# Attention values for two heads at once: 512 columns, one buffer of transposed probabilities

## The chip, the core and the metric

The kernel runs on one core of one Trainium2 chip. The metric is the device time of one execution in microseconds. TensorE (PE) multiplies matrices, VectorE (DVE), ScalarE (ACT) and GpSimd (POOL) compute element by element, SyncE (SP) issues most DMA transfers. PSUM holds the products of TensorE, in eight banks of 128 partitions x 512 fp32; SBUF holds everything else on the chip, DRAM the rest.

## The reference

One layer of an encoder, for two sequences (`s` = 0 and 1) of 1024 positions with 1024 features. The part around the change is latent attention with four heads: scores from a part without position and a rotary part, a softmax over 1024 keys, and the product with the values. Its output and that of a Fourier branch go through one projection, are added to the input, normalised, and feed a feed-forward network.

```python
sc = (jnp.einsum('bqhd,bkhd->bhqk', qn_b, k_nope)
      + jnp.einsum('bqhr,bkr->bhqk', qp_b, k_pe)).astype(jnp.float32) * scale
p = jax.nn.softmax(sc, axis=-1).astype(v.dtype)
return jnp.einsum('bhqk,bkhd->bqhd', p, v)
...
mix = jnp.concatenate([y_mla, y_four], axis=-1) @ w_out
x = x + ga1 * mix
h2 = rmsnorm(x, g_ffn) * (1.0 + sc2) + sh2
ffn = (jax.nn.silu(h2 @ w_gate) * (h2 @ w_up)) @ w_down
```

## The kernel before

A number is split into a high and a low part of type fp32r (`split`, L61: ScalarE casts to the high part at L62, VectorE subtracts it to give the low part at L63), and a product is made of three matmuls: high x high, high x low, low x high (`mm3`, L78, L79, L80). The key and value projections are folded into the queries and into the output weights, so that the values of a head are products with the common latent `ckv` of 128 features.

The stage of the change is the loop over `k` at the end of the attention part. `items` has 64 entries (s, b, h, u): sequence, block of 256 queries (`b`, four in a sequence), head, half of the block (`u`, 128 queries). So eight iterations make one block. An iteration issues:

- `scores(k)`: ten matmuls of 512 columns into two PSUM banks (`ps_s`, two buffers), the maximum on VectorE (L1012), the exponential on ScalarE (L1015), the scaling by the inverse sum (L1017). The result is `p`.
- at fixed places of the eight, the queries of the next block: `rope_q`, `rope_flip` (tile `pqt`), `absorb_q` (tile `qa`), six matmuls of 256 columns each for the first and last;
- `flip_p(k - 1)`: eight transposes of 128 columns (L1033) into two PSUM buffers (`tbank`, tile `ppt`), each split into the transposed probabilities `pt`. `pt` has two parts (high, low) of eight chunks of keys x 256 queries of one head, in two buffers each;
- `values`, in every second iteration, for the head whose halves were flipped: 24 matmuls of 256 columns into `po` (tile `gb`, two buffers of one bank shared with the queries and the output products), split into `o`;
- `out_step`, from k = 11 on, for the block that is finished, by `i` = 0 to 7: loads of two times 128 rows of `fo_d` (the Fourier branch with the input added, `out_load`), four output products of 12 matmuls of 512 columns (`out_proj`, i = 0 to 3), each added by VectorE (L945), the store of the sum and its normalisation (`norm2`, i = 1 and 3), and the transposition of the normalised rows into `h2_d` (`flip_h`, tile `pht`, i = 3 and 5), which takes the same two `tbank` buffers and eight operations on ScalarE (L975);
- the entries of `todo`: the splits of the output weights `wv` (k = 3 to 10 for the first sequence, 39 to 42 for the second), accumulating transfers of the input into `fo_d` on POOL's queue (`add_x`), combinations for the next stage (`comb_h`, k = 49 to 59), loads.

The last two blocks are handled apart: the output products of block (1, 2) are issued in iterations 64 to 67, those of block (1, 3) in the next stage, behind the last values.

The order of each engine's instructions isn't that of the text alone. The program is laid out by a scheduler that plays the engines through with assumed durations: instructions stand in the order in which it finds them ready, with those of earlier iterations first. So transposes whose source isn't ready let later products go ahead. `issue_after` and `first` put single operations behind others.

Of the kernel before, what the change touches and what calls it, by code (L numbers as in the profile page):

```python
# [12 lines left out]
F32 = mybir.dt.float32  # L13
F32R = mybir.dt.float32r
# [7 lines left out]
P = 128  # L22
# [12 lines left out]
NOUT = 6  # L35
# [17 lines left out]
def hybrid_encoder_kernel(ctx: ExitStack, tc: tile.TileContext, a: dict):  # L53
    nc = tc.nc

    here = {}

    def rd(t):
        return t.bitcast(F32)

    def split(hi, lo, src):  # L61
        here["a"] = nc.scalar.copy(hi, src).ins  # L62
        here["v"] = nc.vector.tensor_tensor(out=lo, in0=src, in1=rd(hi), op=ALU.subtract).ins  # L63
# [13 lines left out]
    def mm3(out, lh, ll, rh, rl, first, last, cont=False):  # L77
        nc.tensor.matmul(out, lh, rh, start=first, stop=False, skip_group_check=cont)  # L78
        nc.tensor.matmul(out, lh, rl, start=False, stop=False, skip_group_check=cont)  # L79
        nc.tensor.matmul(out, ll, rh, start=False, stop=last, skip_group_check=cont)  # L80
# [83 lines left out]
    with ExitStack() as st:  # L164
        p1b = st.enter_context(ExitStack())
        w2 = p1b.enter_context(tc.tile_pool(name="p1b", bufs=1, side="right", reuse_waits="tile"))
        w = st.enter_context(tc.tile_pool(name="p1", bufs=1, reuse_waits="tile"))
# [444 lines left out]
    S = {}  # L612
# [65 lines left out]
    def absorb_q(s, b, h, bankf):  # L678
        ql = S["q", s, b]
        pq = bankf()  # L680
        hs = slice(h * P, h * P + P)
        for c in range(2):
            mm3(pq[:, :256], wq_h[:, c, hs], wq_l[:, c, hs], ql[0][:, c, :], ql[1][:, c, :], c == 0, c == 1)
        qa = qa_tiles()
        split(qa[0], qa[1], pq[:, :256])
        S["qa", s, b, h] = qa
# [21 lines left out]
    with ExitStack() as st:  # L708
        early = st.enter_context(ExitStack())
        wa = early.enter_context(tc.tile_pool(name="p2a", bufs=1, reuse_waits="tile"))  # L710
        w = st.enter_context(tc.tile_pool(name="p2", bufs=1, side="right", reuse_waits="tile"))
# [175 lines left out]
        for s in range(2):  # L887
            for n in range(8):
                g, j = n // 4, (1, 2, 3, 0)[n % 4]
# [31 lines left out]
    tail = ExitStack()  # L921
    tl = tail.enter_context(tc.tile_pool(name="p4", bufs=1, side="right", reuse_waits="tile"))
# [6 lines left out]
    def tbank(name, dt=F32):  # L929
        return tl_ps.tile([P, 4, P], dt, tag="t", name=name, bufs=2)  # L930

    def out_load(s, b, u):
        r0 = (2 * b + u) * P
        x2 = tl.tile([P, D], F32, tag="x2", name="x2", bufs=2)
        nc.sync.dma_start(x2, fo_d[s][r0 : r0 + P, :])
        S["x2", s, b, u] = x2

    def out_proj(s, b, u, g):
        o, x2 = S["o", s, b], S["x2", s, b, u]
        us = slice(u * P, u * P + P)  # L940
        gs = slice(512 * g, 512 * g + 512)
        pm = gbank()
        for h in range(HEADS):
            mm3(pm, o[0][:, h, us], o[1][:, h, us], wv[0][:, h, gs], wv[1][:, h, gs], h == 0, h == HEADS - 1)
        here["v"] = nc.vector.tensor_tensor(out=x2[:, gs], in0=x2[:, gs], in1=pm, op=ALU.add).ins  # L945

    def norm2(s, b, u, pool, later=False):
        r0 = (2 * b + u) * P
        x2 = S.pop(("x2", s, b, u))
        (nc.gpsimd if (s, b) == (1, 2) else nc.sync).dma_start(x2_d[s][r0 : r0 + P, :], x2)  # L950
        ms = tiny.tile([P, 2], F32, name="ms2")
        xn = pool.tile([P, D], F32, tag="xn", name="xn", bufs=1)
        sq = nc.scalar.activation(xn, x2, AF.Square, scale=1.0 / 32.0, accum_out=ms[:, 0:1]).ins
        r = rstd(ms[:, 0:1], 1)
        S["xn", s, b, u] = xn

        def scale():
            here["n"] = sq, nc.vector.tensor_scalar(out=xn, in0=x2, scalar1=r[:, 0:1], scalar2=None, op0=ALU.mult).ins

        if later:  # L960
            S["scale"] = scale
        else:
            scale()

    def flip_h(s, b, u):
        r0 = (2 * b + u) * P
        xn = S.pop(("xn", s, b, u))
        for g in range(2):
            ht = tl.tile([P, 4, P], F32, tag="ht", name="ht", bufs=2)
            pt = tbank("pht")  # L970
            for c in range(4):
                nc.tensor.transpose(pt[:, c, :], xn[:, (4 * g + c) * P : (4 * g + c + 1) * P], ident)
            for c in range(4):
                cc = 4 * g + c
                nc.scalar.activation(ht[:, c, :], pt[:, c, :], AF.Identity,  # L975
                                     bias=sh2[s][:, cc : cc + 1], scale=s2[s][:, cc : cc + 1])
            nc.sync.dma_start(h2_d[s][:, 4 * g : 4 * g + 4, r0 : r0 + P], ht)

    def out_step(s, b, i):
        if i == 0:  # L980
            out_load(s, b, 0)
            out_load(s, b, 1)
        if i < 4:
            out_proj(s, b, i // 2, i % 2)
        if i in (1, 3):
            norm2(s, b, i // 2, tl, True)
        if i in (3, 5):
            flip_h(s, b, i // 4)

    with ExitStack() as st:  # L990
        w = st.enter_context(tc.tile_pool(name="p3", bufs=1, side="right", reuse_waits="tile"))
# [28 lines left out]

        def flip_p(s, b, h, u):
            p = S.pop(("p", s, b, h, u))
            if (s, b, h, u) == (0, 0, 0, 0):
                w.tile([P, 8], F32, name="phase_pt")
            if u == 0:
                S["pt", s, b, h] = [w.tile([P, 8, 2, P], F32R, tag=f"pt{k}", name=f"pt{k}", bufs=2) for k in range(2)]
            if (s, b, h, u) == (0, 0, 0, 0):
                w.tile([P, 120], F32, name="phase_l")
            pth, ptl = S["pt", s, b, h]
            for g in range(2):  # L1030
                pt = tbank("ppt")
                for c in range(4):
                    nc.tensor.transpose(pt[:, c, :], p[:, (4 * g + c) * P : (4 * g + c + 1) * P], ident)  # L1033
                split(pth[:, 4 * g : 4 * g + 4, u, :], ptl[:, 4 * g : 4 * g + 4, u, :], pt)

        def values(s, b, h):
            ckv = S[s][1]
            pth, ptl = S.pop(("pt", s, b, h))
            if h == 0:
                S["o", s, b] = [tl.tile([P, HEADS, 256], F32R, tag=f"o{i}", name=f"o{i}b{s}{b}", bufs=3) for i in range(2)]  # L1040
            o = S["o", s, b]
            po = gbank()
            for c in range(8):
                mm3(po[:, :256], ckv[0][:, c, :], ckv[1][:, c, :], pth[:, c], ptl[:, c], c == 0, c == 7)
            split(o[0][:, h, :], o[1][:, h, :], po[:, :256])

        items = [(s, b, h, u) for s in range(2) for b in range(4) for h in range(HEADS) for u in range(2)]
        nit = len(items)
# [48 lines left out]
        for k in range(nit + 4):  # L1097
            if k >= nit:
                i = k - nit
                out_proj(1, 2, i // 2, i % 2)  # L1100
                S["tail", i] = here["v"]
                if i == 1:
                    norm2(1, 2, 0, tl)
                    S["tail", 5], S["tail", 6] = here["n"]
            if k < nit:
                s, b, h, u = items[k]
                scores(s, b, h, u)
                if "scale" in S:
                    with tc.issue_after(here["nb"]):
                        S.pop("scale")()  # L1110
                if k == nit - 1:
                    with tc.issue_after(here["exp"]):
                        nc.scalar.activation(tiny.tile([P, 1], F32, tag="pc", name="warm"), cmask[:, 0:1], AF.Silu)
                nxt = items[k + 8 - k % 8] if k + 8 - k % 8 < nit else None
                i = k % 8
                if nxt is not None:
                    if i == 0:
                        load_q(*nxt[:2])
                    if i == 3 and nxt[1] == 0:
                        load_seq(nxt[0], [w.tile([P, 2, N], F32R, tag=f"lat1{i}", name=f"lat1{i}") for i in range(2)])  # L1120
                    if i in (3, 4):
                        rope_q(*nxt[:2], i - 3, gbank)
                    if i in (5, 6):
                        rope_flip(*nxt[:2], i - 5, tbank("pqt", F32R))
                if u == 1 and k + 1 < nit:
                    absorb_q(*items[k + 1][:3], gbank)
            if 0 <= k - 1 < nit:
                flip_p(*items[k - 1])
                if k == nit:
                    S["tail"] = here["a"], here["v"]  # L1130
            if 0 <= k - 3 < nit and (k - 3) % 2 == 1:
                values(*items[k - 3][:3])
                if k == nit + 2:
                    S["tail", 4], S["tail", 7] = here["v"], here["a"]
            m = k - 11
            if 0 <= m < 8 * NOUT:
                out_step(*divmod(m // 8, 4), m % 8)
            for f in todo.get(k, ()):
                f()

    with ExitStack() as st:
# [171 lines left out]
        for s in range(2):  # L1313
# [241 lines left out]
            m, me = {}, {}  # L1555
# [223 lines left out]
```

## Time and profile before

| | |
|---|---|
| median of 3 runs | 2050.19 us (2047.45 to 2050.26) |
| the profiled execution | 2048.8 us, of which its span 2047.0 |
| granted TensorE clock, mean | 0.993 |
| TensorE busy | 1989.8 us (97%) |
| VectorE, ScalarE, GpSimd busy | 1416.4, 902.3, 835.3 us |
| attention stage, first scores to last values | 313.98 to 743.89 us |

A row of the profile's groups has the line, the engine, the operation, output and inputs by the program's names, shapes and the count; then busy time, the mean of one in ns, and the engine's idle time before them with what ended it. A row in order of time has start, duration, engine, line and what it makes. Busy times by stretch have for each engine the time and in brackets the number of operations, then the granted clock, the share of the DMA engines and what they moved.

### The profile page before, as it was taken

How to read it: one execution, taken by the hardware profiler on the slowest of the kernel's cores; microseconds unless marked ns; L12 is line 12 of the kernel's file. 1: busy time of each engine (PE TensorE's matmuls, PEld its weight loads, DVE VectorE, ACT ScalarE, POOL GpSimd, SP SyncE). 2: the span in 40 equal slices, each digit the busy share in tenths (PEclk: the TensorE clock that was granted, in tenths of full speed). 3: DMA queues.
4: the chain of work that ended last, by engine and by line, in shares of the span. 5: the costliest groups of instructions: out<-in, count | busy, mean ns of one | idle time of the engine just before them, and what ended most of it. 6: DMA issues, size and time to landing. Idle time of an engine off the chain costs nothing.

```text
span 2047.0 us, 28668 instructions
## 1 busy us (share of the span) xinstructions
PE 1989.8 (97%) x9994; PEld 1650.2 (81%) x9994; DVE 1416.4 (69%) x2098; ACT 902.3 (44%) x1761; POOL 835.3 (41%) x1026
## 2 busy tenths in 40 slices
PE   5999999999999999999999999999999999999997
PEld 2788878888888887888888888877788888888876
DVE  2667757666677669878777576677766666667674
ACT  2656635555565555333333365454233333336441
POOL 1455213111313316879779410332654454410142
PEclk7999999999999999999999999999999999999999
DMA  9685694544643465546546587674432222358662
GB/s 368 204 268 188 216 341 138 128 87 104 170 104 121 157 240 200 192 156 219 187 159 210 170 295 258 214 233 148 135 113 103 99 107 103 103 186 276 225 224 88
DMA packets 182509, 370.36 MB, mean 181 GB/s; under 512 B 18972, under 2 KB 58396, under 8 KB 179292
## 3 DMA queue, kind: packets, MB, share of 16 engines
q1 hardware_dynamic: 163228, 308.88, 45.1%
q0 software_dynamic: 19136, 59.65, 9.7%
q8 instruction: 78, 1.28, 0.3%
q14 instruction: 67, 0.55, 0.1%
HBM read 256.46 MB, written 120.39 MB: 184 GB/s over the span
## 4 chain that ended last, share of the span: by engine, by line
PE 53%; DVE 3%; DMA 2%; issue 1%; POOL 1%; ACT 0%; SPq 0%; DVEq 0%; ACTq 0%; POOLq 0%
PE bank L79 18%; PE bank L78 18%; PE bank L80 18%; DVE wl L63 2%; DVE val L138 1%; DMA draw<-t_d 1%; POOL val L138 0%; ACT wh L62 0%; DMA rgu<-in_wgu_dram 0%; DVE val L1578 0%; POOL rs_y L106 0%; DMA draw<-s_d 0%; DVE val L1552 0%; DMA draw<-in_w_down_dram 0%; DMA val<-x_d 0%
## 5 line engine op out<-in xcount | busy, mean ns | idle before, releaser
L78 PE MATMUL bank<-H,wh 128*128 128x512 f32 x1224 | 477.4, 390 | 7.1 <-DVE val L138 6.4
L80 PE MATMUL bank<-H,wl 128*128 128x512 f32 x1224 | 476.4, 389 | 0.2 <-DVE wl L63 0.2
L79 PE MATMUL bank<-H,wh 128*128 128x512 f32 x1224 | 476.2, 389 | 0.0
L138 DVE TENSOR_TENSOR val<-bank,val 128x512 f32<-128x512 f32 x244 | 166.7, 688 | 162.0 <-PE bank L80 157.8
L78 PEld LDWEIGHTS bank<-H,wh 128*128 128x128 f32 x1224 | 229.8, 188 | 58.4 <-DVE val L138 7.3
L80 PEld LDWEIGHTS bank<-H,wl 128*128 128x128 f32 x1224 | 229.8, 188 | 49.1 <-DVE wl L63 1.5
L79 PEld LDWEIGHTS bank<-H,wh 128*128 128x128 f32 x1224 | 229.8, 188 | 47.2
L63 DVE TENSOR_TENSOR wl<-draw,wh 128x512 fp32r<-128x512 f32 x286 | 203.4, 744 | 84.9 <-ACT wh L62 84.6
L62 ACT CAST wh<-draw 128x512 fp32r<-128x512 f32 x286 | 169.4, 621 | 158.6 <-PE bank L79 85.3
L79 PE MATMUL bank<-wl,wh 128*128 128x512 f32 x572 | 223.8, 391 | 2.7 <-DVE wl L63 2.7
L138 POOL TENSOR_TENSOR val<-val 128x512 f32<-128x512 f32 x58 | 83.0, 1440 | 347.6 <-DVE val L1552 191.3
L78 PE MATMUL bank<-wh 128*128 128x512 f32 x572 | 222.7, 389 | 0.1
L80 PE MATMUL bank<-wh,wl 128*128 128x512 f32 x572 | 222.7, 389 | 0.0
L62 ACT CAST wh<-rgu 128x512 fp32r<-128x512 f32 x171 | 106.5, 624 | 249.2 <-PE bank L79 195.1
L63 DVE TENSOR_TENSOR wl<-val,wh 128x512 fp32r<-128x512 f32 x133 | 140.5, 1058 | 71.7 <-ACT wh L62 71.3
L63 DVE TENSOR_TENSOR wl<-rgu,wh 128x512 fp32r<-128x512 f32 x171 | 170.0, 995 | 6.9 <-ACT wh L62 6.9
L62 ACT CAST wh<-val 128x512 fp32r<-128x512 f32 x133 | 82.5, 623 | 181.0 <-PE bank L79 156.4
L135 POOL TENSOR_TENSOR val<-rgu 128x512 f32<-128x512 f32 x80 | 112.7, 1409 | 98.0 <-DMA rgu<-in_wgu_dram 94.3
L79 PEld LDWEIGHTS bank<-wl,wh 128*128 128x128 f32 x572 | 107.4, 188 | 28.6 <-DVE wl L63 6.7
L78 PEld LDWEIGHTS bank<-wh 128*128 128x128 f32 x572 | 107.4, 188 | 23.0 <-ACT wh L62 0.7
L80 PEld LDWEIGHTS bank<-wh,wl 128*128 128x128 f32 x572 | 107.4, 188 | 22.1
L1012 DVE TENSOR_REDUCE mx<-ps_s 128x1 f32<-128x1024 f32 x64 | 78.2, 1222 | 61.3 <-PE ps_s L1007 60.8
(385 smaller groups left out, 4092.2 us busy)
## 6 DMA issues: line engine op xcount, KB each, us to landing
rgu<-in_wgu_dram SPq DMA_DIRECT2D x86, 512.0 KB
draw<-s_d SPq DMA_DIRECT2D x143, 256.0 KB
s_d<-val POOLq DMA_DIRECT2D x88, 256.0 KB, 4.2
draw<-t_d SPq DMA_DIRECT2D x88, 256.0 KB
s_d<-val SPq DMA_DIRECT2D x66, 256.0 KB
draw<-in_w_down_dram SPq DMA_DIRECT2D x55, 256.0 KB
wada<-in_w_ada_dram SPq DMA_DIRECT2D x13, 1024.0 KB
xt<-in_x_dram SPq DMA_DIRECT2D x16, 512.0 KB
```

What stands on the lines that cost most here:

```text
L62: here["a"] = nc.scalar.copy(hi, src).ins
L63: here["v"] = nc.vector.tensor_tensor(out=lo, in0=src, in1=rd(hi), op=ALU.subtract).ins
L78: nc.tensor.matmul(out, lh, rh, start=first, stop=False, skip_group_check=cont)
L79: nc.tensor.matmul(out, lh, rl, start=False, stop=False, skip_group_check=cont)
L80: nc.tensor.matmul(out, ll, rh, start=False, stop=last, skip_group_check=cont)
L135: return eng.tensor_tensor(out=out, in0=x, in1=y, op=ALU.subtract).ins
L138: return eng.tensor_tensor(out=out, in0=x, in1=y, op=ALU.add).ins
L1012: nc.vector.tensor_reduce(out=mx, in_=ps, axis=AX.X, op=ALU.max)
```

## The change

`values` takes two heads (`q` = 0 or 1, heads 2q and 2q + 1) at once. A pair's transposed probabilities have four tiles, high and low for each half `g` of the keys, each of four chunks x 512 columns (two heads x two halves), with one buffer each instead of two: the same memory as before. Its 24 matmuls have 512 columns and fill a whole PSUM bank; there are half as many. They are issued where k mod 4 is 1, ahead of `flip_p`, so that the products of a pair stand before the first flip of the next pair. The output steps of a block, which took eight iterations in a row, are spread over i = 9 to 19, counted from the block's own first iteration: loads at 9 and 11, products at 10, 12, 15 and 16, normalisations at 12 and 16, flips at 14 and 19. None of the products falls on an iteration with values. Two small tiles that only moved addresses go away.

```diff
     def out_step(s, b, i):
-        if i == 0:
-            out_load(s, b, 0)
-            out_load(s, b, 1)
-        if i < 4:
-            out_proj(s, b, i // 2, i % 2)
-        if i in (1, 3):
-            norm2(s, b, i // 2, tl, True)
-        if i in (3, 5):
-            flip_h(s, b, i // 4)
+        if i in (9, 11):
+            out_load(s, b, i // 2 - 4)
+        if i in (10, 12, 15, 16):
+            n = (10, 12, 15, 16).index(i)
+            out_proj(s, b, n // 2, n % 2)
+        if i in (12, 16):
+            norm2(s, b, i // 4 - 3, tl, True)
+        if i in (14, 19):
+            flip_h(s, b, int(i == 19))
...
         def flip_p(s, b, h, u):
             p = S.pop(("p", s, b, h, u))
-            if (s, b, h, u) == (0, 0, 0, 0):
-                w.tile([P, 8], F32, name="phase_pt")
-            if u == 0:
-                S["pt", s, b, h] = [w.tile([P, 8, 2, P], F32R, tag=f"pt{k}", name=f"pt{k}", bufs=2) for k in range(2)]
-            if (s, b, h, u) == (0, 0, 0, 0):
-                w.tile([P, 120], F32, name="phase_l")
-            pth, ptl = S["pt", s, b, h]
+            if h % 2 == 0 and u == 0:
+                S["pt", s, b, h // 2] = [[w.tile([P, 4, 4, P], F32R, tag=f"pt{k}{g}", name=f"pt{k}{g}", bufs=1) for k in range(2)]
+                                         for g in range(2)]
+            i = 2 * (h % 2) + u
             for g in range(2):
+                pth, ptl = S["pt", s, b, h // 2][g]
                 pt = tbank("ppt")
                 for c in range(4):
                     nc.tensor.transpose(pt[:, c, :], p[:, (4 * g + c) * P : (4 * g + c + 1) * P], ident)
-                split(pth[:, 4 * g : 4 * g + 4, u, :], ptl[:, 4 * g : 4 * g + 4, u, :], pt)
-
-        def values(s, b, h):
+                split(pth[:, :, i, :], ptl[:, :, i, :], pt)
+
+        def values(s, b, q):
             ckv = S[s][1]
-            pth, ptl = S.pop(("pt", s, b, h))
-            if h == 0:
+            pts = S.pop(("pt", s, b, q))
+            if q == 0:
                 S["o", s, b] = [tl.tile([P, HEADS, 256], F32R, tag=f"o{i}", name=f"o{i}b{s}{b}", bufs=3) for i in range(2)]
-            o = S["o", s, b]
+            o = [t[:, 2 * q : 2 * q + 2, :].rearrange("p h t -> p (h t)") for t in S["o", s, b]]
             po = gbank()
             for c in range(8):
-                mm3(po[:, :256], ckv[0][:, c, :], ckv[1][:, c, :], pth[:, c], ptl[:, c], c == 0, c == 7)
-            split(o[0][:, h, :], o[1][:, h, :], po[:, :256])
+                pth, ptl = (t[:, c % 4].rearrange("p i t -> p (i t)") for t in pts[c // 4])
+                mm3(po, ckv[0][:, c, :], ckv[1][:, c, :], pth, ptl, c == 0, c == 7)
+            split(o[0], o[1], po)
...
+            if (k % 4 == 1 and 5 <= k < nit) or k == nit + 2:
+                values(*divmod(k // 8 - (k % 8 == 1), 4), k // 4 % 2 ^ 1) if k < nit else values(1, 3, 1)
+                if k == nit + 2:
+                    S["tail", 4], S["tail", 7] = here["v"], here["a"]
             if 0 <= k - 1 < nit:
                 flip_p(*items[k - 1])
                 if k == nit:
                     S["tail"] = here["a"], here["v"]
-            if 0 <= k - 3 < nit and (k - 3) % 2 == 1:
-                values(*items[k - 3][:3])
-                if k == nit + 2:
-                    S["tail", 4], S["tail", 7] = here["v"], here["a"]
-            m = k - 11
-            if 0 <= m < 8 * NOUT:
-                out_step(*divmod(m // 8, 4), m % 8)
+            for n in (k // 8 - 1, k // 8 - 2):
+                if 0 <= n < NOUT:
+                    out_step(*divmod(n, 4), k - 8 * n)
```

How the order of instructions moves is shown at three places. First TensorE, around the values of the third head of the first block (before). `gb` is the product, `pt` the transposed probabilities, `ppt` a transposition, `ps_s` scores:

```order
L1007 MATMUL ps_s<-lat_3363,qp 128x512
L78 MATMUL gb<-pt_3962,ckv_3385 128x256
L79 MATMUL gb<-pt_3963,ckv_3385 128x256
L80 MATMUL gb<-pt_3962,ckv_3386 128x256
L78 MATMUL gb<-pt_3962,ckv_3385 128x256
L1033 MATMUL ppt<-ident,p 128x128 x8
L79 MATMUL gb<-pt_3963,ckv_3385 128x256
L80 MATMUL gb<-pt_3962,ckv_3386 128x256
```

The same engine with the change, at the end of the values of heads 2 and 3 of that block:

```order
L78 MATMUL gb<-pt_3962,ckv_3385 128x512
L79 MATMUL gb<-pt_3963,ckv_3385 128x512
L80 MATMUL gb<-pt_3962,ckv_3386 128x512
L1031 MATMUL ppt<-ident,p 128x128 x8
L1003 MATMUL ps_s<-lat_3362,qa_4147 128x512
L1004 MATMUL ps_s<-lat_3363,qa_4147 128x512
```

Before, the transposes of the next half stood inside the run of value products; now they stand behind it, ahead of scores.

Second ScalarE, near a run of values. Before, late in the stage (`o0b` is the cast of the values, `pt` that of the transposed probabilities, `p` the exponential, `qa` a query):

```order
L1015 ACTIVATE p,sm<-ps_s,nb 128x1024
L62 CAST o0b_8236<-gb 128x256
L62 CAST qa_8295<-gb 128x256
L62 CAST pt_8299<-ppt 128x4x128 x2
L1015 ACTIVATE p,sm<-ps_s,nb 128x1024
L62 CAST pt_8299<-ppt 128x4x128 x2
L1015 ACTIVATE p,sm<-ps_s,nb 128x1024
```

With the change, in the second block:

```order
L1015 ACTIVATE p,sm<-ps_s,nb 128x1024
L62 CAST o0b_4438<-gb 128x512
L62 CAST pt_4736<-ppt 128x4x128
L62 CAST pt_4738<-ppt 128x4x128
L62 CAST pt_4736<-ppt 128x4x128
L62 CAST pt_4738<-ppt 128x4x128
L1015 ACTIVATE p,sm<-ps_s,nb 128x1024
```

Behind the cast of the values there now stand the casts of two flips in a row, of the first two items of the next pair, and then the next exponential.

Third TensorE, around the flip of normalised rows (`pht`). Before (`gb<-wv` are output products):

```order
L79 MATMUL gb<-wv_3638,o0b_3892 128x512
L80 MATMUL gb<-wv_3637,o1b_3893 128x512
L972 MATMUL pht<-ident,xn 128x128 x8
L1003 MATMUL ps_s<-lat_3362,qa_4519 128x512
L1004 MATMUL ps_s<-lat_3363,qa_4519 128x512
L1005 MATMUL ps_s<-lat_3362,qa_4520 128x512
```

With the change (`gb<-wq` are query products):

```order
L972 MATMUL pht<-ident,xn 128x128 x4
L78 MATMUL gb<-wq_h,ql_4630 128x256
L79 MATMUL gb<-wq_l,ql_4630 128x256
L972 MATMUL pht<-ident,xn 128x128 x4
L80 MATMUL gb<-wq_h,ql_4631 128x256
L78 MATMUL gb<-wv_3637,o0b_4438 128x512
L79 MATMUL gb<-wv_3638,o0b_4438 128x512
L80 MATMUL gb<-wv_3637,o1b_4439 128x512
L78 MATMUL gb<-wv_3637,o0b_4438 128x512
L1031 MATMUL ppt<-ident,p 128x128 x4
```

The two halves of this flip stood together, with all scores of an iteration behind them; now query products lie between them, and transposes of probabilities follow after four output products.

## The prediction

> **What bounds the kernel now.** I read the page first, then busy time by stretch, then the TensorE groups and the order of time in the stage that is changed.
>
> ```profile
> span 2047.0 us, 28668 instructions
> PE 1989.8 (97%) x9994; PEld 1650.2 (81%) x9994; DVE 1416.4 (69%) x2098; ACT 902.3 (44%) x1761; POOL 835.3 (41%) x1026
> PEclk7999999999999999999999999999999999999999
> PE 53%; DVE 3%; DMA 2%; issue 1%; POOL 1%; ACT 0%; SPq 0%; DVEq 0%; ACTq 0%; POOLq 0%
> ```
>
> TensorE is busy all the time, at a full granted clock after the first slice, and the chain that ended last is made of TensorE. The change lies in the attention stage, the 64 iterations of the loop over `items`. From its first scores at 313.98 us to the last product of values at 743.89 us it takes 429.9 us. Busy time by stretch (the 11 first iterations; two times 8 of the middle; the 8 where the second sequence sets in; the last):
>
> ```profile
> core 0: us, PE busy (x) PEld busy (x) DVE busy (x) ACT busy (x) POOL busy (x), PEclk, DMA share, GB/s
> 313.98:370.62 56.64, 54.43 (x337) 47.34 (x336) 46.11 (x85) 32.20 (x61) 15.56 (x16) 0.97 0.40 108
> 394.50:449.70 55.20, 54.99 (x349) 48.90 (x348) 36.62 (x71) 30.04 (x64) 8.40 (x20) 1.00 0.43 97
> 449.70:504.90 55.20, 54.99 (x349) 48.90 (x348) 36.63 (x71) 30.04 (x64) 8.46 (x20) 1.00 0.43 97
> 574.69:631.49 56.80, 55.87 (x351) 48.77 (x350) 41.26 (x79) 33.79 (x73) 8.99 (x21) 1.00 0.46 112
> 694.95:743.89 48.94, 48.35 (x311) 43.18 (x310) 34.25 (x59) 26.71 (x51) 8.99 (x12) 1.00 0.63 230
> ```
>
> Eight iterations cost 55.20 us, with VectorE busy for 36.6 of them. A busy TensorE is not yet a TensorE at its pace, since matmuls overlap: one that is listed with 0.39 us is followed by the next after 0.23. So I count by starts (first and last of a run of equal products).
>
> ```profile
> 433.32 0.39 PE L1003 MATMUL ps_s<-lat,qa 128*128 128x512 f32 x1
> ...
> 435.36 0.39 PE L1007 MATMUL ps_s<-lat,qp 128*128 128x512 f32 x1
> ...
> 436.31 1.03 PE L1033 MATMUL ppt<-ident,p 128*128 128x128 f32 x8
> 437.10 0.37 PE L78 MATMUL gb<-pt,ckv 128*128 128x256 f32 x1
> 437.30 0.28 PE L79 MATMUL gb<-pt,ckv 128*128 128x256 f32 x1
> ...
> 439.89 0.28 PE L80 MATMUL gb<-pt,ckv 128*128 128x256 f32 x1
> ```
>
> Nine steps of 512 columns take 2.04 us, 0.227 us each; 22 steps of 256 columns take 2.59 us, 0.1177 each. Eight transposes take 0.79 us to the next product, which then is 0.08 us longer than usual: 0.87 us. For 8 iterations of the middle that is 80 scores (18.1 us), 96 value products (11.3), 48 output products (10.9), 80 transposes (8.7), 36 query products of 256 columns (4.2) and two small flips (0.7): 54.0 us. The other 1.2 us of the 55.20 are waits of TensorE. Where they are, in order of time:
>
> ```profile
> 462.67 0.28 PE L80 MATMUL gb<-ql,wq_l 128*128 128x256 f32 x1
> 462.79 0.60 PE L1033 MATMUL ppt<-ident,p 128*128 128x128 f32 x4
> 463.14 0.36 PE L78 MATMUL gb<-pt,ckv 128*128 128x256 f32 x1
> 463.56 0.66 PE L1033 MATMUL ppt<-ident,p 128*128 128x128 f32 x4
> ```
>
> One value product starts at 463.14, and the four transposes behind it start 0.42 us later instead of 0.12. They had been put into a run of value products, and their source or their PSUM buffer wasn't ready.
>
> **The change part by part.**
>
> *512 columns.* The value products:
>
> ```profile
> L78 PE MATMUL gb<-pt,ckv 128*128 128x256 f32 x256 | 73.4, 287 | 0.0
> L80 PE MATMUL gb<-pt,ckv 128*128 128x256 f32 x256 | 72.6, 283 | 0.0
> L79 PE MATMUL gb<-pt,ckv 128*128 128x256 f32 x256 | 72.4, 283 | 0.0
> ```
>
> 768 of these become 384 with 512 columns. Two small ones step 0.2354 us, a large one 0.227: 0.0084 x 384 = 3.2 us less, all of it on TensorE, which is the path. The Trainium skill (TensorE: Matmul & The Clock Gate, Back-to-back issue gap) gives a warm gap of columns / 2.4 + 2.5 ns; an estimate by it is 2.5 ns saved for each pair, 1.0 us in all, and the sum would be 2.2 us smaller. The measured steps are 8 to 11 ns above that rule, so I keep the rows.
>
> *Waits inside the value products.* In the order, the transposes no longer stand in a run of value products; now a whole run of 24 stands by itself and the transposes behind it. In the middle 1.2 us per 8 iterations are waits, over 6.6 such stretches (11 to 63) 7.9 us. I take half of this, 4.0 us, as gone. Why not all: the flips of the normalised rows (`pht`) share two PSUM buffers (`tbank`) with those of the probabilities, and they move into iterations 3 and 6 of 8, where both kinds follow each other closely. Each of these flips keeps ScalarE for eight operations.
>
> ```profile
> L975 ACT ACTIVATE ht<-pht,sh,s 128x128 f32<-128x128 f32 x16 | 5.9, 469 | 2.9 <-PE pht L972 2.8
> L62 ACT CAST pt<-ppt 128x512 fp32r<-128x512 f32 x16 | 8.9, 596 | 7.9 <-PE ppt L1033 7.8
> L1012 DVE TENSOR_REDUCE mx<-ps_s 128x1 f32<-128x1024 f32 x8 | 9.8, 1223 | 9.9 <-PE ps_s L1007 9.8
> L63 DVE TENSOR_TENSOR pt<-ppt,pt 128x512 fp32r<-128x512 f32 x17 | 11.2, 683 | 0.5 <-ACT pt L62 0.3
> ```
>
> 16 of them busy ScalarE for 5.9 us, 0.37 each. In the order of before, scores and a query product (3.0 us) lie between a flip and the next transposes; now 1.7 to 2.4 us do, and four of these operations alone take 1.5. So I expect about 0.2 us of wait for each of two flips in 8 iterations, 2.6 us of the 7.9 over the stage, and a little beside. Bounds: all 7.9 go, or they double (+7.9).
>
> *One buffer of transposed probabilities.* The first flip of the next pair may be written only after the value products have read the pair before. It stands behind them on TensorE anyway, so its cast is never ready earlier: cost 0. The other side is the products' own wait for the last flip before them: a cast (0.596 us), a subtraction (0.683). Between the two the order puts output products and scores (12 x 0.227 + 10 x 0.227 = 5.0 us); that is the cover. In the first ten iterations only scores and a query product are there, about 2 us, and I expect a few tenths. Without cover each of the 16 pairs would cost up to 1.28 us.
>
> *Output products and their DMAs.* Their number stays. Loads of `fo_d` rows move from i = 0 (k = 8n + 11) to k = 8n + 9 and 8n + 11, the stores of `x2_d` and `h2_d` move back, on SP's queue. The first load needs the second accumulating transfer of POOL's queue:
>
> ```profile
> 361.16 0.89 POOL L622 DMA_DIRECT2D fo_d<-in_x_dram  x1
> 368.40 0.81 SPq L935 DMA_DIRECT2D x<-fo_d  x2
> ```
>
> SP waits there until 368.40, and the first addition on VectorE would now come some 3 us earlier than before. At worst it waits for the load, with a split of `wv` and the next maximum behind it, while TensorE has scores: 0 to 2 us once, I take 0. The second split of `wv` (iterations 39 to 42) now follows the last output products of sequence 0 at once; its casts stand behind those of the flips on ScalarE, so nobody waits. Where it used to meet iterations without any product, 56.80 us stood for 55.20. I don't count that 1.6 us, it is in the range.
>
> *The end.* The last split of values is now twice as large:
>
> ```profile
> 744.09 0.38 ACT L62 CAST o0b<-gb 128x256 fp32r<-128x256 f32 x1 [3.65 <-PE gb L80]
> 744.50 0.42 DVE L63 TENSOR_TENSOR o1b<-gb,o0b 128x256 fp32r<-128x256 f32 x1 [0.34 <-ACT o0b L62]
> 744.84 0.68 DVE L135 TENSOR_TENSOR H<-rgu 128x512 f32<-128x512 f32 x1
> ```
>
> VectorE goes straight on with the sums for the next stage, and TensorE waits for it there later. With 0.596 and 0.683 in place of 0.38 and 0.42 this is 0.5 us more. The 12 output products behind the last value products (2.7 us) still hide it from the projection of the last block.
>
> *Sum:* -3.2 - 4.0 + 0.5 = -6.7 us. The profiled execution took 2048.8 us: 2042.1. The median shown is 1.4 us above that execution, so for a median I say 2043.5.
>
> **The rivals.**
>
> *Only the columns count.* The waits go from value products to flips and stay 7.9 us. For it: they come from VectorE's and ScalarE's chain, which loses little work, and the order is planned with other durations than the chip's. Against it: the runs of 24 give 5.4 us in one piece in which both engines catch up. Time: -3.2 + 0.5 = -2.7, 2047.5.
>
> *The single buffer stops TensorE.* Slower. If a cast of the new pair stands first in ScalarE's queue, waiting for the value products, the exponentials behind it wait too; and if the products wait for the last cast and subtraction, all 16 pairs pay 1.28 us, 20.5 us: -2.7 + 20.5 = +17.8, 2068. It decides as soon as less than 1.28 us of TensorE work lies between the last flip of a pair and the first value product. The Trainium skill (TensorE: Matmul & The Clock Gate, Architectural detail) calls ScalarE's and VectorE's queues strictly first in, first out; this speaks against the change. Against this rival: in the order 5.0 us lie there, and the exponential of the scores ahead of the products stands before the waiting casts, not behind them. A milder form, flips that wait 1.0 us each in place of 0.2, twice in 8 iterations, costs 6.6 x 1.6 = 10.6 us above the forecast: 2054.
>
> *The handover eats it.* The next stage begins with waits on VectorE; if its loads, not the end of attention, set them, some of the 6.7 are lost. They shift with the stage, since their buffers are freed by it. Time: between 2044 and 2050, with the first rival.
>
> That the program doesn't do it is no rival: the order shows the runs of 24 with 512 columns and the output products spread.
>
> **How the numbers follow.** About 0.2% (4.1 us) is what a measurement of this kernel can tell from no change. Forecast (2038 to 2046): 0.60. Only the columns, or the gain lost in the handover (2046 to 2054): 0.27. Slower by either form of the single-buffer or flip waits: 0.13. Lower end: all 7.9 and the 1.6 go: -3.2 - 9.5 + 0.5 = -12.2, 2038; I give 2037. Upper end 2053, where the slower case begins; that leaves about 0.15 above and a little below.
>
> **What would show it.** The value products: x128 for each of L78, L79 and L80, steps of 0.227 us. Scores of the middle, 8 iterations apart: 54.2 us instead of 55.2. No transposes inside a run of value products; ScalarE's and VectorE's waits for TensorE at flips about the same. Wrong would be: 8 iterations still at 54.8 or more (the first rival), or value products that start over 0.5 us after the product ahead of them, or scores that wait for an exponential behind a cast of `pt` (the second). If the stage is 6 us shorter and the whole is not, it is the handover.

## The result, and the profile after

The changed kernel takes 2043.61 us (median of 20 runs, 2040.12 to 2047.32), the kernel before 2047.76 in the same rounds (20 runs, 2044.37 to 2051.33): ratio 0.9979, 95% interval 0.9973 to 0.9986, so 4.15 us less (2.9 to 5.5). The forecast was 2043.5 for a median of 2050.19, 6.7 us less. The kernel before came out 2.4 us lower in these rounds than the median on which the forecast was built, so the figures to compare are 4.15 and 6.7. The profiled execution after took 2042.28 us.

The page after: span, busy time, granted clock, shares of the chain.

```profile
span 2040.5 us, 27843 instructions
PE 1982.0 (97%) x9610; PEld 1626.2 (80%) x9610; DVE 1407.8 (69%) x2082; ACT 897.3 (44%) x1745; POOL 835.7 (41%) x1026
PEclk7999999999999999999999999999999999999999
PE 54%; DVE 2%; DMA 2%; POOL 1%; issue 1%; ACT 1%; SPq 0%; DVEq 0%; ACTq 0%; POOLq 0%
```

TensorE is the bound as before, with 384 matmuls less and the same clock. Busy time by stretch of the changed kernel, for the first 11 iterations, eight of the middle and the eight where the second sequence sets in:

```profile
core 0: us, PE busy (x) PEld busy (x) DVE busy (x) ACT busy (x) POOL busy (x), PEclk, DMA share, GB/s
314.01:371.24 57.23, 54.98 (x301) 45.75 (x300) 46.30 (x85) 32.54 (x62) 16.01 (x16) 1.00 0.42 114
446.79:501.48 54.69, 54.69 (x303) 46.03 (x302) 35.88 (x68) 29.49 (x63) 8.43 (x20) 1.00 0.42 96
568.79:623.46 54.67, 54.67 (x301) 46.03 (x300) 40.39 (x78) 33.47 (x70) 8.75 (x20) 1.00 0.48 116
```

The first 11 iterations take 57.23 us for 56.64, because output products now fall into them that came later before. Eight iterations of the middle, with the same work, take 54.69 us for 55.20, only 0.51 less; where the second sequence sets in, 54.67 for 56.80, which is 2.1 less. The value products by group (busy time and mean of one in ns; the other two lines are alike):

```profile
L79 PE MATMUL gb<-pt,ckv 128*128 128x512 f32 x128 | 50.0, 390 | 0.0
```

and the start of one run in order of time:

```profile
467.16 0.40 PE L78 MATMUL gb<-pt,ckv 128*128 128x512 f32 x1
...
469.68 0.39 PE L80 MATMUL gb<-pt,ckv 128*128 128x512 f32 x1
```

Eleven steps in 2.52 us, 0.229 each, and no transposes between them. What TensorE waits for in the attention stage by semaphores, before and then after (in total, times, longest):

```profile
PE ppt L1033 <- DVE nb L1013: 1.8, 1, 1.8
PE ppt L1033 <- DVE p L1017: 1.1, 6, 0.2
PE ps_s L1005 <- DVE qa L63: 1.0, 2, 0.5
PE ps_s L1003 <- ACT qa L62: 0.5, 1, 0.5
PE gb L78 <- DVE qt L663: 0.3, 1, 0.3
```

```profile
PE ppt L1031 <- DVE nb L1013: 2.3, 2, 1.6
PE pht L972 <- DVE pt L63: 1.8, 1, 1.8
PE ppt L1031 <- DVE pt L63: 0.7, 1, 0.7
PE ps_s L1003 <- ACT p L1015: 0.4, 1, 0.4
```

The many small waits of transposes for `p` are gone; one long wait of a flip (`pht`) is new. The view leaves out short delays, so I also split the whole stage, from the first scores to the last value product, by the starts of all of TensorE's instructions. Expected steps are 0.2268 us for 512 columns and 0.1177 for 256, transposes with the late start of the product behind them as they come; what a step takes beyond that is slow up to 0.115 us and a wait above:

| kernel or experiment (one profile each) | stage, us | expected | slow steps | waits | groups of transposes |
|---|---|---|---|---|---|
| before | 429.8 | 414.8 | 3.2 | 11.8 | 90 |
| after | 424.2 | 411.2 | 4.3 | 8.6 | 109 |
| after, second profile | 426.2 | 412.0 | 4.3 | 9.9 | 109 |
| `narrow` | 430.3 | 415.4 | 6.2 | 8.8 | 109 |
| `spread` | 435.7 | 414.4 | 4.1 | 17.3 | 89 |
| `pairs` | 428.0 | 410.4 | 5.4 | 12.1 | 98 |
| `comb53` | 422.2 | 411.4 | 4.5 | 6.4 | 109 |
| `flips1520` | 422.8 | 410.7 | 4.2 | 7.9 | 87 |
| `allthree` | 419.1 | 410.5 | 5.5 | 3.2 | 80 |
| `held` | 418.1 | 410.3 | 5.3 | 2.5 | 80 |

In the stage expected steps are 3.6 us fewer and waits 3.2 us fewer, and slower steps take back 1.1: 5.6 us, up to rounding. A second profile of the same kernel has 2 us more in the stage, most of it waits in its first iterations: by it the stage gains 3.6 us and its waits 1.9. So one profile tells a stage to about 2 us, and the 6.5 us between the two spans is more than the 4.15 of the medians.

### The profile page after: what moved, and what is told of

Its sections match the earlier page's. It is cut to its first block, busy times and chain, and to the rows that moved or that the text cites. A ratio compares the mean times of both kernels' runs of the same rounds, so it can differ in the third digit from the quotient of the medians.

```text
span 2040.5 us, 27843 instructions
## 1 busy us (share of the span) xinstructions
PE 1982.0 (97%) x9610; PEld 1626.2 (80%) x9610; DVE 1407.8 (69%) x2082; ACT 897.3 (44%) x1745; POOL 835.7 (41%) x1026
## 4 chain that ended last, share of the span: by engine, by line
PE 54%; DVE 2%; DMA 2%; POOL 1%; issue 1%; ACT 1%; SPq 0%; DVEq 0%; ACTq 0%; POOLq 0%
PE bank L78 18%; PE bank L79 18%; PE bank L80 18%; DVE wl L63 1%; DMA draw<-s_d 1%; DMA draw<-t_d 1%; DMA val<-x_d 1%; DVE val L138 0%; ACT wh L62 0%; POOL val L138 0%; DVE val L1577 0%; DMA rgu<-in_wgu_dram 0%; POOL rs_y L106 0%; SPq L1537 0%; DVE val L135 0%
## 5 line engine op out<-in xcount | busy, mean ns | idle before, releaser
L138 POOL TENSOR_TENSOR val<-val 128x512 f32<-128x512 f32 x58 | 84.4, 1462 | 343.4 <-DVE val L1551 187.0
L63 DVE TENSOR_TENSOR wl<-val,wh 128x512 fp32r<-128x512 f32 x133 | 145.2, 1093 | 72.1 <-ACT wh L62 71.8
L135 POOL TENSOR_TENSOR val<-val 128x512 f32<-128x512 f32 x89 | 119.3, 1359 | 1.3
```

What stands on the lines that cost most here:

```text
L135: return eng.tensor_tensor(out=out, in0=x, in1=y, op=ALU.subtract).ins
L138: return eng.tensor_tensor(out=out, in0=x, in1=y, op=ALU.add).ins
```

## The experiments

Ratios are to the kernel before in the same rounds, with 95% intervals. My theory was the forecast's: columns and undisturbed runs of value products. The rivals: only the columns count, or the spreading does the work.

### Columns alone: `narrow`

```diff
-            for c in range(8):
-                pth, ptl = (t[:, c % 4].rearrange("p i t -> p (i t)") for t in pts[c // 4])
-                mm3(po, ckv[0][:, c, :], ckv[1][:, c, :], pth, ptl, c == 0, c == 7)
+            for j in range(2):
+                js = slice(256 * j, 256 * j + 256)
+                for c in range(8):
+                    pth, ptl = (t[:, c % 4].rearrange("p i t -> p (i t)") for t in pts[c // 4])
+                    mm3(po[:, js], ckv[0][:, c, :], ckv[1][:, c, :], pth[:, js], ptl[:, js], c == 0, c == 7)
```

> The changed kernel with each value block of 512 columns computed in two passes of 24 matmuls with 256 columns; all else stays, the order too. By the forecast's first term (steps of 0.1177 us in place of 0.227) it is 3.2 us slower than the changed kernel, 2046.8 us, and 0.95 of the 4.15 us gained are left. By the Trainium skill (TensorE: Matmul & The Clock Gate, Back-to-back issue gap) an estimate is 1.0 us slower, 2044.6. If the gain came from the order and not from the columns, it stays at 2043.6.

2049.83 us beside 2050.08, ratio 0.9999 (0.9991 to 1.0008). Set against 0.9979, the columns are worth about 4 us (2 to 6) in this order, all of the gain. The 3.2 us of the forecast's first term, which would give 0.9995, lie within this interval; 1.0 us (0.9985) and nothing (0.9979) don't. In order of time, a run of 256 columns behind query products:

```profile
470.32 0.28 PE L80 MATMUL gb<-ql,wq_l 128*128 128x256 f32 x1
470.44 0.28 PE L78 MATMUL gb<-pt,ckv 128*128 128x256 f32 x1
...
472.24 0.28 PE L78 MATMUL gb<-pt,ckv 128*128 128x256 f32 x1
```

Fifteen steps in 1.80 us: 0.120 each, not the 0.1177 of the forecast. From start to start all value products take 92.2 us here and 87.5 in the changed kernel. The 4.7 us are more than the 3.2 of the forecast and far from its estimate of 1.0 us by the Trainium skill's gap of columns / 2.4 + 2.5 ns (TensorE: Matmul & The Clock Gate, Back-to-back issue gap); these matmuls, each with weights of its own, don't follow it. The page calls this gap that of a matmul by itself.

The place of a run doesn't explain its step. All sixteen runs of `narrow` step 0.120, also the one that stands directly behind transposes:

```profile
715.94 0.64 PE L1031 MATMUL ppt<-ident,p 128*128 128x128 f32 x4
716.34 0.37 PE L78 MATMUL gb<-pt,ckv 128*128 128x256 f32 x1
716.54 0.28 PE L79 MATMUL gb<-pt,ckv 128*128 128x256 f32 x1
...
722.06 0.28 PE L80 MATMUL gb<-pt,ckv 128*128 128x256 f32 x1
```

From 716.54 to 722.06 there are 46 steps in 5.52 us, 0.120 each. In the kernel before, undisturbed runs step 0.1165 to 0.1179, also the last one, which stands behind output products:

```profile
740.86 0.39 PE L80 MATMUL gb<-wv,o1b 128*128 128x512 f32 x1
741.09 0.28 PE L78 MATMUL gb<-pt,ckv 128*128 128x256 f32 x1
...
743.77 0.28 PE L80 MATMUL gb<-pt,ckv 128*128 128x256 f32 x1
```

Here 23 steps take 2.68 us, 0.117 each. Why 256 columns step 0.120 in `narrow` and 0.117 before, no run shows. So `narrow` isn't a perfect control: it says that this order gains nothing without the wide products, but about 2 us of the difference (768 steps that are 0.0023 to 0.003 us longer) come from this step. Without it, by this estimate, the order alone would be worth up to 2 us. By the table `narrow` saves 3.0 us of waits and loses 3.0 to slower steps, 1.8 of them these.

### Each half of the change alone: `spread` and `pairs`

`spread` is the kernel before with the output steps moved as in the change. Of the diff, the output products and the loop (loads, normalisations and flips move to the same iterations as in the change):

```diff
...
-        if i < 4:
-            out_proj(s, b, i // 2, i % 2)
+        if i in (10, 12, 15, 16):
+            n = (10, 12, 15, 16).index(i)
+            out_proj(s, b, n // 2, n % 2)
...
-            m = k - 11
-            if 0 <= m < 8 * NOUT:
-                out_step(*divmod(m // 8, 4), m % 8)
+            for n in (k // 8 - 1, k // 8 - 2):
+                if 0 <= n < NOUT:
+                    out_step(*divmod(n, 4), k - 8 * n)
```

> The kernel before with the output steps spread over other iterations alone; one head per value block with 256 columns and two buffers stay. In its order transposes still stand inside the runs of value products (30 places; 25 before, 15 at other places after). If spreading is worth something by itself, it takes the 0.95 us that the columns don't explain: 2046.8. If that rest comes from taking transposes out of the value runs, spreading alone gives nothing: 2047.8, or a little more, up to 2049, since VectorE now waits for GpSimd's rstd.

2058.16 us, ratio 1.0040 (1.0027 to 1.0053): 8 us slower, which neither expectation had. What TensorE waits for:

```profile
PE ppt L1033 <- DVE p L1017: 6.4, 6, 2.2
PE ps_s L1005 <- DVE qa L63: 2.1, 6, 0.4
```

and the second longest of these places in order of time:

```profile
648.93 0.28 PE L78 MATMUL gb<-pt,ckv 128*128 128x256 f32 x1
651.05 1.06 PE L1033 MATMUL ppt<-ident,p 128*128 128x128 f32 x8 [1.84 <-DVE p L1017]
```

Transposes still stand in the runs of value products and stop there for VectorE's scale. I read it so, without a run of its own: the twelve output products that gave VectorE time ahead of such a place are now elsewhere.

`pairs` is the changed kernel with the output steps of before (the same diff backwards).

> The changed kernel with the output steps of before (iterations 11 to 16 of a block of 8), that is, pairs of heads with 512 columns and one buffer alone. No transposes in the value runs. If the gain is columns plus undisturbed runs (the forecast's steps 1 and 2), it stands at the changed kernel, 2043.6, or 1 to 2 us below, since the waits of flips at 530.29 (0.86 us) and 651.71 (1.97 us) belong to the spread normalisation. If spreading is needed to cover the waits of the one buffer, it is slower than the changed kernel, 2045 to 2048.

2050.23 us, ratio 0.9995 (0.9986 to 1.0004). The worse branch of the expectation: pairs of heads bring the columns and lose them again to waits (12.1 us for 8.6). The largest group is scores that wait for the cast of their absorbed query on ScalarE:

```profile
PE ps_s L1003 <- ACT qa L62: 2.8, 6, 0.5
PE ppt L1031 <- DVE nb L1013: 2.4, 3, 1.8
```

So neither half gains by itself (+8 us, and -1 us that is not clear of zero), and both together gain 4.

### The new wait of a flip: `comb53`

In the changed kernel TensorE stops at 651.71 us; TensorE, then VectorE and GpSimd at that place:

```profile
651.71 0.28 PE L80 MATMUL gb<-wq_h,ql 128*128 128x256 f32 x1
653.80 0.66 PE L972 MATMUL pht<-ident,xn 128*128 128x128 f32 x4 [1.80 <-DVE pt L63]
...
650.22 1.52 DVE L1017 TENSOR_SCALAR p<-p,rr 128x1024 f32<-128x1024 f32 x1
651.65 1.48 DVE L667 TENSOR_TENSOR qsk<-qt,qsk 128x256 fp32r<-128x256 f32 x1
...
649.89 1.29 POOL L138 TENSOR_TENSOR hcb<-hca 128x512 f32<-128x512 f32 x1
651.14 1.71 POOL L135 TENSOR_TENSOR hcb<-hca 128x512 f32<-128x512 f32 x1
```

VectorE's two operations end just behind GpSimd's (651.74 behind 651.18, 653.13 behind 652.85), and the `pt` split that frees the flip's PSUM buffer comes late.

```diff
-        for c, k in enumerate((49, 51, 57, 59)):
+        for c, k in enumerate((49, 53, 57, 59)):
```

> The changed kernel with one group of GpSimd sums (comb_h of c = 1) put in iteration 53 in place of 51. If these sums slow VectorE's scale and subtraction (1.5 us each) and so hold the flip of normalised rows for 1.97 us, that wait goes and the time is 2041.6 us. If the flip waits for something else, or the sums meet VectorE as badly in iteration 53, it stays at 2043.6.

The same two operations of VectorE with GpSimd's sums elsewhere, and TensorE at the flip:

```profile
651.38 0.76 DVE L1017 TENSOR_SCALAR p<-p,rr 128x1024 f32<-128x1024 f32 x1
652.04 0.42 DVE L667 TENSOR_TENSOR qsk<-qt,qsk 128x256 fp32r<-128x256 f32 x1
...
652.87 0.28 PE L80 MATMUL gb<-wq_h,ql 128*128 128x256 f32 x1
653.12 0.66 PE L972 MATMUL pht<-ident,xn 128*128 128x128 f32 x4
```

0.76 and 0.42 us in place of 1.52 and 1.48, and the flip starts 0.25 us after the product ahead of it, not 2.09. The cause of this wait is shown. The whole takes 2044.55 us, ratio 0.9969 (0.9957 to 0.9981): 2 us below the changed kernel's, but the intervals overlap.

### The flips elsewhere: `flips1520`

```diff
...
-        if i in (14, 19):
-            flip_h(s, b, int(i == 19))
+        if i in (15, 20):
+            flip_h(s, b, int(i == 20))
```

> The changed kernel with the flips of the normalised rows at iterations 15 and 20 of a block in place of 14 and 19. In its order all eight transposes of such a flip stand together behind twelve output products, and the transposes stand in 90 groups, not 112. Theory one, a group of transposes costs next to nothing by itself (the last transpose steps 0.028 us, the product behind it 0.315, together a transpose and a product) and only the waits count: the 1.97 us at 651.71 goes, about 1 us for second groups that start 0.05 us slower: 2040.6 to 2041.6 us. Theory two, each group costs the 0.09 us that the product behind it is late, and more: 22 x 0.13 = 2.9 us besides: 2038.7. Theory three, the forecast's fear of the flips: only 2.3 us of scores now lie between a flip and the next transposes, while eight operations of ScalarE take 3.0; each of 12 flips waits 0.5 to 1 us: 2048 to 2054.

2043.91 us beside 2050.46, ratio 0.9961 (0.9947 to 0.9976); stage 1.4 us shorter, which is less than two profiles of one kernel differ. The time alone excludes only theory three, my fear of the forecast (no flip waits here); theories one and two both lie within the interval (0.9965 to 0.9970 and 0.9956). The trace speaks against theory two: 22 groups fewer should have brought 2.9 us, and the steps expected with them fell by 0.5. Theory one is wrong on the long wait: in this kernel too GpSimd's sums stand in iteration 51, and the wait is still there, only at other transposes:

```profile
PE ppt L1031 <- DVE nb L1013: 2.9, 2, 2.4
PE ppt L1031 <- DVE pt L63: 2.3, 3, 1.5
```

### The first iterations: `wv5`, `allthree` and `held`

`wv5` is `comb53` with one more move:

```diff
-            todo[2 * g].append(lambda g=g: gate_half(0, g))
-            todo[2 * g].append(lambda g=g: wv_load(0, g))
+            todo[5 * g].append(lambda g=g: gate_half(0, g))
+            todo[5 * g].append(lambda g=g: wv_load(0, g))
```

> As the run with the GpSimd sums in iteration 53, and the second half of the first sequence's output weights is loaded and multiplied on GpSimd in iteration 5, not 2. Theory: GpSimd's multiplications slow VectorE's scale of the probabilities (1.75 us at 329.54 where others take 0.76), and TensorE waits 1.82 us for it at 329.40; that wait goes, and the kernel is 1.8 us below the run with the sums in iteration 53: ratio to the kernel before near 0.996, 2039.8 us beside 2047.8. Rival: the wait is the start of the loop, where only scores and queries are there to cover it, and stays; or the multiplications hold a scale elsewhere: no change.

2045.69 us, ratio 0.9978 (0.9966 to 0.9989). It tells nothing of its theory: the scheduler let the multiplications run at 329.23 to 334.86 us, 12.8 us behind the first scores, as in `comb53` (12.7). It does tell how far nearly equal kernels lie apart: 0.0009 from `comb53`.

`allthree` adds to `wv5` the flips at 15 and 20 and takes `rope_flip` out of its place ahead of the transposes:

```diff
...
-                    if i in (5, 6):
-                        rope_flip(*nxt[:2], i - 5, tbank("pqt", F32R))
...
+            if k < nit and nxt is not None and i in (5, 6):
+                rope_flip(*nxt[:2], i - 5, tbank("pqt", F32R))
             for n in (k // 8 - 1, k // 8 - 2):
```

> As the run before, with the flips of the normalised rows at 15 and 20 and the two flips of the rotary queries behind the transposes of the probabilities, not ahead. 83 groups of transposes. If the gains add up: the wait of 1.97 us is gone already, the flips give about 1 us, the rotary flips free both PSUM buffers for the eight transposes (the waits of 0.24 us in iterations 7 of 8, 8 times: 2 us): 3 us below the run before, some 2037 us beside 2047.8. If the flips at 15 and 20 wait for ScalarE, it is 5 us or more above the run before.

2041.63 us, ratio 0.9954 (0.9939 to 0.9969), stage 2.5 us below the 421.6 of `wv5`; the waits of 0.24 us in front of a second group of four transposes are gone. `held` is `allthree` and puts GpSimd's multiplications where they were meant to be:

```diff
+            mark = None
+            if (s, g) == (0, 1):
+                pc = tiny.tile([P, 1], F32, name="pc")
+                mark = nc.gpsimd.tensor_tensor(out=pc, in0=S["rr"], in1=S["rr"], op=ALU.add).ins
...
-                nc.gpsimd.tensor_tensor(out=raw, in0=raw, in1=S["ga"], op=ALU.mult)
+                with tc.issue_after(mark) if mark else ExitStack():
+                    nc.gpsimd.tensor_tensor(out=raw, in0=raw, in1=S["ga"], op=ALU.mult)
```

> As the run with all three, and GpSimd's second group of multiplications of output weights (L1071 of the changed kernel) is held behind the inverse sum of iteration 5. The run before, which only moved its loads to iteration 5, left the multiplications where they were (329.23 to 334.86 us), so it told nothing. Theory: VectorE's scale of the probabilities runs at half its pace beside GpSimd's multiplications (1.75 us for 0.75), and TensorE waits for it 1.85 us at 328.63; held, that wait shrinks by the 1.0 us that the scale is shorter, to about 0.85, and the stage is 1 us shorter. Rival one: the wait is VectorE's queue at the start of the loop and stays at 1.85. Rival two: the multiplications hold the scale of a later iteration, ahead of the first values, and a new wait of 1 us comes there.

TensorE and VectorE at the first wait, in `allthree`:

```profile
328.63 0.40 PE L1004 MATMUL ps_s<-lat,qa 128*128 128x512 f32 x1
330.71 0.52 PE L1031 MATMUL ppt<-ident,p 128*128 128x128 f32 x3 [1.68 <-DVE nb L1013]
...
328.81 1.75 DVE L1017 TENSOR_SCALAR p<-p,rr 128x1024 f32<-128x1024 f32 x1
```

and in `held`:

```profile
328.89 0.40 PE L1004 MATMUL ps_s<-lat,qa 128*128 128x512 f32 x1
329.93 0.74 PE L1031 MATMUL ppt<-ident,p 128*128 128x128 f32 x5 [0.64 <-DVE nb L1013]
...
329.05 0.74 DVE L1017 TENSOR_SCALAR p<-p,rr 128x1024 f32<-128x1024 f32 x1
```

The scale is 1.01 us shorter, and the gap between the two starts falls from 2.08 to 1.04 us: a wait of 0.81, where 0.85 was expected. 0.40 us come back at 344.24, so the second rival is right in part. The whole: 2038.35 us, ratio 0.9954 (0.9942 to 0.9966), the same ratio as `allthree`: the 1 us of the stage can't be seen in it. Its attention stage as a stretch, columns as above:

```profile
313.80:731.88 418.08, 416.83 (x2283) 352.15 (x2281) 295.88 (x544) 235.98 (x473) 100.08 (x164) 1.00 0.50 135
```

### The changed kernel again

> The changed kernel as it is, for a comparison with the run before on one chip. The traces of the variants give the attention stage 424.2 us in the changed kernel and 419.1 with all three moves; if the times follow the stage, the changed kernel is 5 to 6 us above the held run here, ratio 0.998 to the kernel before; if the two stand closer than 3 us, the stage's gain is lost behind it.

2045.66 us, ratio 0.9982 (0.9974 to 0.9991), on the same chip as `held` with 2038.35. The interval of `held` lies wholly below, as does that of `allthree`: this version beats both kernels, the changed one by some 6 us by the ratios, as expected.

## Why the prediction was right, point by point

*The time.* By the gain it came out between the forecast's 6.7 us and the first rival's 2.7: 4.15 (2.9 to 5.5), nearer to the rival. That the absolute time agrees to 0.1 us is luck, since the kernel before stood 2.4 us lower.

*512 columns (-3.2).* The mechanism was right: without the wide products nothing is left of the gain. Its size is known only roughly. By the steps of the kernel before (0.1165 to 0.1179, and 0.2277 for the wide ones after) it is 2 to 3 us, by the trace of `narrow` 4.7 on the value products, by its whole 4 us with 2 either way. The difference is the step of 0.120 in place of 0.117, whose cause is open. The forecast took one step, 0.1177, from one run, and that lies at the upper end of its kernel's runs.

*Waits in the value products (-4.0).* This is the term that failed. Waits did fall, by 3.2 us in one profile and 1.9 in the other, but 1.1 came back as slower steps, and of 4.15 us the columns leave no more than about 2 for it, by `narrow` nothing. "The other 1.2 us of the 55.20 are waits of TensorE" is the step that failed: by starts, 0.67 us are waits in the eight iterations (the 0.42 us shown at 463.14 hold 0.2 of wait, since a product behind transposes steps 0.20 anyway), the rest is transposes in groups that begin slowly and products that step 0.231 and not 0.227. So the 54.2 us forecast for eight iterations became 54.69, close to the 54.8 at which the first rival would have been taken. 1.5 us of the waits saved come from a place that I hadn't counted: where the second sequence sets in, 1.8 us of waits became 0.3. This is the 1.6 us that the forecast left out of its sum.

*Left out: slower steps (+1.1).* Products of 512 columns that now stand behind transposes, where products of 256 stood, step 0.231 us for about ten products. No run here shows the cause; it stays open.

*The first rival* was half right: with the columns taken away nothing is left of the gain, since in `narrow` the waits saved are lost to slower steps. But the waits didn't go to flips in its way. *Flips at 0.2 us each*: five waited 0.13 to 0.18 us, and one 1.97, and that not because of ScalarE, which the forecast blamed, but because of GpSimd's sums beside VectorE. Together they make 2.7 us; that this is next to the forecast's 2.6 is luck.

*The single buffer (0).* Right: no value product appears among the waits after. *Output loads (0 to 2)*: TensorE waits for none. What I had not looked at is the normalisation, which now stands behind GpSimd's chain on VectorE's queue:

```profile
DVE xn L958 <- POOL rs_r L110: 22.4, 13, 5.5
```

It was 3.1 us before; nearly all of it is hidden.

*The end (+0.5).* The last split takes 0.59 and 0.69 us as forecast. From the last value product to the end there are 1303.3 us before, 1302.3 after, 1304.0 in the second profile, and 1302.4 to 1305.4 in the variants; half a microsecond can't be seen in that. In the first profile the handover kept the gain; a loss of one or two microseconds there is within the spread and isn't excluded.

## What to carry to other kernels

Don't price a wider matmul by the step of one run: 0.003 us in the narrow step, 768 times, is most of the term. Take the step from many runs, and build the narrow form in the new order as a control. Where TensorE is nearly always busy, separate waits from slow steps by the starts before calling the rest of a stretch a wait: here the waits shrank with the new order and the slow steps grew. And when one of VectorE's short operations sometimes takes twice its time, look at what GpSimd began just ahead of it, and move that.

## What the runs showed of the hardware

VectorE's scale of 128x1024 fp32 takes 0.75 us alone and up to 1.80 in the changed kernel (1.88 in `pairs`) beside GpSimd's element-wise operations, its subtraction of 128x256 1.48 for 0.42; the maximum over PSUM takes 1.22 us either way. The Trainium skill (SBUF — State Buffer, SBUF: two separate sides) calls the pair of ports of the two engines an exclusive lock that the first holds for its whole instruction; of VectorE's operations it names those in a two-port mode or with two inputs in SBUF. The rows agree: the subtraction has two inputs in SBUF, the maximum none, and what counts is who starts first. In all six places of the changed kernel's stage where one of GpSimd's operations of 512 columns begins ahead of the scale, the scale ends 0.55 to 0.56 us after that operation, however early it began itself; the subtraction at 651.65 ends 0.28 us after. Where the scale begins first, as in `held` at 341.14 us, it takes 0.79 us, and GpSimd's multiplication behind it 1.73 for 1.28. That 0.55 and 0.28 are less than the 0.75 and 0.42 of an undisturbed operation isn't explained by any run.

A group of transposes costs almost nothing at its edge: the last transpose steps 0.028 us and the product behind it 0.315, together 0.343, where a transpose and a product take 0.109 and 0.227.
